# Low parts of four weight blocks made on GpSimd at their first use, and two gate products moved behind the fourth pair of heads

## The chip, the cores and the metric

The kernel runs on one core of a Trainium2 chip. The metric is the device time of one execution in microseconds (us). The core has five engines that work side by side, each through its own queue in order: TensorE (PE in the profile, PEld for its weight loads), VectorE (DVE), ScalarE (ACT), GpSimd (POOL) and SyncE (SP), which here issues nearly all DMA transfers.

## The reference

A two-layer trunk over 1024 frames of 1024 channels. Cut to what matters here:

```python
def s5_mixer(u, ..., glu_w, glu_b):
    ...
    y = jax.nn.gelu(y)
    y = y * jax.nn.sigmoid(y @ glu_w + glu_b)
    return y

def mixer_ab(h, w_in, ..., w_out):
    proj = h @ w_in
    u_s5, g_s5, q, k, v, g_ret = jnp.split(proj, cuts, axis=-1)
    y_s5 = s5_mixer(u_s5, ...) * jax.nn.silu(g_s5)
    y_ret = retention(q, k, v) * jax.nn.silu(g_ret)
    return jnp.concatenate([y_s5, y_ret], axis=-1) @ w_out

def mixer_conv(h, w_in, conv_w, conv_b, ln_g, ln_b, w_out):
    a, b, g = jnp.split(h @ w_in, 3, axis=-1)
    u = a * jax.nn.sigmoid(b)
    ...
```

Layer 0 is `x = x + mixer_ab(rmsnorm(x))`, layer 1 is `x = x + mixer_conv(rmsnorm(x))`, and a last rmsnorm follows. Retention normalises each head over its 128 channels: `(out - mu) * rsqrt(var + EPS)`. All is float32.

## The kernel before

**Products in three parts.** Every large product of float32 matrices is made as three passes over numbers split in a high and a low part: high x high, high x low, low x high (lines 277, 278 and 279, function `mm3`). A weight block of 1024 x 128 so needs two tiles, `wh` (a rounding copy, made by ScalarE) and `wl` (the rest, `wf - wh`). A pass of TensorE is one block of weights against one half `h` of the frames (512): 8 x 3 = 24 matmuls of 128 x 512 into one bank of PSUM. Three banks serve these passes in turn (`ps_mm`). A pass can begin when the bank of three passes before has been read.

**Where `wl` comes from.** The list `wseq` (function `plan`) names all weight blocks in the order of use; `wnext` hands out the next one and starts the loads of two more. `wload` then has three ways: `wload_pieces` loads `wf`, casts it on ScalarE (L268) and subtracts on GpSimd or VectorE (L269); `wload_again` loads `wf`, casts it (L146) and loads `wl` ready made from DRAM (L155); a third makes sums. Layer 1's blocks `cb0` to `cb7` and `ca0` to `ca7` (the halves b and a of `w_in`) are each used twice, once for each half of the frames. Their low parts are made beforehand and kept in DRAM (`lo_cb..`, `lo_ca..`), so both uses go by `wload_again`. `weight_low` makes half of such a block: load 256 KB (`lf`), cast on ScalarE (`lh`, L233), subtract (L234), store 256 KB (L237). There are 32 halves, numbered k = 0 to 31; k // 4 is the number of the block pair, so k = 0 to 7 are cb0, ca0, cb1 and ca1. Eighteen (`LOWS`) are made on GpSimd during the first three pairs of retention heads, and fourteen on VectorE in the gate stage behind the fourth pair: two after each pass (nb, 0) with nb of 2 to 6, one after each (nb, 1) with nb of 2 to 5. There they use two buffers in turn.

**The stage around the change.** `ret_heads` treats the retention heads in four pairs: the products of scores and values (`ro`, L1170 and L1174), statistics and roots on VectorE and ScalarE (L1183, L1184, L558, L559), normalised tiles `on` (L1194), transposes on TensorE (`rt`, L1200), and the products with the retention gate (`grl`, L1205; the last one is `last_turn`). The fourth pair lies among the first passes of the S5 gate (`mm_glu`): the order of TensorE there is written by hand. The passes run (0,0), (1,0), (0,1), (1,1), then (2,0), (2,1) to (5,1), then (6,0), (7,0), (6,1), (7,1), as (nb, h). For each, GpSimd makes `yg` = gs x yn from two loads (L1281; two buffers), ScalarE takes tanh of the bank (L1294), and VectorE makes `sg` = (sg + 1) x yg (L1298). Operands of these passes are the y tiles that `load_split` casts (L1221) and subtracts (L1223). The matrices of the output projection follow (`w_out_first`), then layer 1 with `ab(0)`: passes cb0, ca0, cb1, ca1 and so on for the first half of the frames (`mm_b`, `mm_a`), then a convolution whose taps are shared between VectorE (L1510) and GpSimd (L1490, products by ScalarE, L1489).

**What sets the order.** Instructions are traced with a priority (the program's order, or `self.at(...)`), and a planner that simulates the engines writes each engine's queue. `tc.issue_after(ins)` puts the instructions of its block behind `ins` in the queue of the engine of `ins`, without a semaphore; `chained` does the same one by one.

Of the kernel before, what the change touches and what calls it, by code (L numbers as in the profile page):

```python
# [33 lines left out]
LO_V = {f"g{i}" for i in range(1, 10)} | {"u4", "u5", "u6"}  # L34
G0 = 3
TP = 6
LOWS = 18
Y_ORDER = tuple(range(8)), (0, 2, 4, 6, 5, 7, 1, 3)
AHEAD = (0, 1, 2)
P_ORDER = ([(1, nb) for nb in range(4)] + [(2, nb) for nb in range(4)] +  # L40
# [18 lines left out]
class Trunk:  # L59
# [61 lines left out]
    def wload(self, src, name):  # L121


        if name[0] == "V":
            return self.wload_value(name)
        if src is None:
            return self.wload_sums(name)
        key, twice = name[:-2], name[:2] in TWICE and name[:-2] + "_1" in self.wnames
        if twice and key in self.lo_d:
            return self.wload_again(src, name, self.lo_d[key])  # L130
        tiles = None
        with self.at(190000) if name == "cg3_0" else nullcontext():
            for tiles in self.wload_pieces(src, name, 1, [self.nc.vector if name[:2] in LO_V or name[:3] in LO_V else self.nc.gpsimd]):
                done = tiles or done
        if twice and name.endswith("_0"):
            self.lo_d[key] = self.dram.tile([P, D], F32, name=f"lo_{key}")
            self.nc.sync.dma_start(self.lo_d[key], done[1][:].rearrange("p k n -> p (k n)").bitcast(F32))
        return done
# [803 lines left out]
    def retention(self, st):  # L942
        nc, A = self.nc, self.A
        r0 = self.r0 = self.pool("ret0", 1, stack=st)
        early = ExitStack()
        rq = self.rq = self.pool("retq", 1, stack=early, side="right")
        self.vt = [[(r0 if d else rq).tile([P, 4, HALF], F32, name=f"v{d}_{h}") for h in range(2)] for d in range(2)]
        self.rk = rq.tile([P, 2, T], F32, name="ropek")
        nc.sync.dma_start(self.rk[:], A["rope_k"])
        for i in range(2):  # L950
            for c in (slice(0, HALF), slice(HALF, T)):
                nc.gpsimd.tensor_tensor(self.rk[:, i, c], self.rk[:, i, c], self.R[:, c], op=ALU.mult)
        self.mask = r0.tile([P, 4, 64], F32, name="retmask")
        nc.sync.dma_start(self.mask[:], A["ret_mask"])
        self.g64 = r0.tile([P, 4], F32, name="g64")
        nc.sync.dma_start(self.g64[:], A["ret_g64"])
        self.kdec = r0.tile([P, NH], F32, name="kdec")
        nc.sync.dma_start(self.kdec[:], A["ret_kdec"])
        self.reps = r0.tile([P, NH], F32, name="reteps")
        nc.sync.dma_start(self.reps[:], A["ret_eps"])  # L960
        first = self.ret_proj(0)
        next(first)
        for pair in range(4):
            if pair == 0:
                with ExitStack() as vst:
                    V = self.ret_values(self.pool("vp", 1, stack=vst))
                self.rp = self.pool("ret", 1, stack=st)
                cur = list(first)[-1]
                self.crossed(0)
                ry = self.pool("retl", 1, stack=early, side="right")  # L970

            def lows(n, behind):
                with self.tc.issue_after(behind.ins):
                    for k in range(n * LOWS // 6, (n + 1) * LOWS // 6) if pair < 3 else ():
                        self.weight_low(ry, k, (("la", "lb"), ("la", "lb")), 3, nc.gpsimd)

            def turned():
                lows(2 * pair + 1, self.last_kt)
                if pair == 3:
                    early.close()  # L980
                    self.lp = self.pool("l1", side="right")
            lows(2 * pair, self.last_rs if pair else self.last_sum)
            ahead = pair in AHEAD and self.ret_proj(pair + 1)
            if ahead:
                next(ahead)
            cur = self.ret_heads(pair, *cur, V, turned, lambda: list(ahead)[-1] if ahead else None)
            if pair < 3:
                self.crossed(pair + 1)
# [229 lines left out]


    def split(self, src, hi, lo, eng, behind=None):  # L1220
        self.nc.scalar.copy(hi[:], src)  # L1221
        with self.tc.issue_after(behind.ins) if behind else nullcontext():
            eng.tensor_tensor(lo[:], src, hi[:].bitcast(F32), op=ALU.subtract)  # L1223

    def layer0_back_and_layer1(self, st):
# [37 lines left out]
        v.tensor_scalar(hgb[:], self.vecs[:, V_GLUB * KB:(V_GLUB + 1) * KB], 0.5, None, op0=ALU.mult)  # L1263
        ys_in = load_split(self.yn_d, "y", False)
        ys0, sg0, t2f, t3f, passes = {}, {}, {}, {}, {}
        left = iter(range(LOWS, 32))

        def lows(n):
            for k in islice(left, n):
                with self.tc.issue_after(self.last_turn.ins), self.tc.issue_after(self.roots[3].ins):  # L1270
                    self.weight_low(lp, k, (("cs", "pilot"), ("cq", "sq")), 1)
        ws = {}

        for nb, h in [(0, 0), (1, 0), (0, 1), (1, 1)] + [(nb, h) for nb in range(2, 6) for h in range(2)] + [(6, 0), (7, 0), (6, 1), (7, 1)]:
            if h == 0:
                ws[nb] = self.wnext(f"glu{nb}")
            yg = lp.tile([P, HALF], F32, name=f"yg{nb}_{h}", tag="ld", bufs=2)
            nc.sync.dma_start(yg[:], self.gs_d[rows(nb), hs(h)])
            yn = lp.tile([P, HALF], F32, name=f"yn{nb}_{h}", tag="ev", bufs=4)
            nc.sync.dma_start(yn[:], self.yn_d[rows(nb), hs(h)])  # L1280
            gp.tensor_tensor(yg[:], yg[:], yn[:], op=ALU.mult)  # L1281
            ps = self.bank(f"mm_glu{nb}_{h}", aux=False)
            for n, kb in enumerate(Y_ORDER[h]):
                behind = {(0, 1, 1): self.last_kv, (1, 1, 0): passes.get((0, 1, 2)), (0, 1, 3): self.last_ro,
                          (1, 1, 2): passes.get((0, 1, KB - 1))}.get((nb, h, n))
                with self.tc.issue_after(behind.ins) if behind else nullcontext():
                    self.mm3(ps[:], ws[nb], kb, (ys_in[h][kb][0][:], ys_in[h][kb][1][:]), n == 0, n == KB - 1)
                passes[nb, h, n] = self.last_mm
                self.after_pass({(0, 0, 4): self.third_turns[0], (1, 0, 2): self.third_turns[2],
                                 (1, 0, 4): self.third_turns[3], (1, 1, 1): self.second_scores, (1, 1, 6): self.turns[0], (2, 0, 5): self.turns[2],  # L1290
                                 (2, 1, 0): self.turns[3]}.get((nb, h, n)))
            sg = lp.tile([P, HALF], F32, name=f"sg{nb}_{h}", tag="u", bufs=5)
            with self.tc.issue_after(self.roots[1].ins) if (nb, h) == (0, 1) else nullcontext():
                last_sg = nc.scalar.activation(sg[:], ps[:], AF.Tanh, scale=0.5, bias=hgb[:, nb:nb + 1])  # L1294
            if nb < 2 and nb != h:
                self.chained([self.roots[2 * h]], last_sg)
            with self.tc.issue_after(self.masked[1].ins):
                v.scalar_tensor_tensor(sg[:], sg[:], 1.0, yg[:], op0=ALU.add, op1=ALU.mult)  # L1298
            if h == 0:
                a, b = (self.op_tile(opB, "B0", f"ys{q}{nb}") for q in "hl")  # L1300
                nc.scalar.mul(a[:], sg[:], 0.5)
                glu_end = v.scalar_tensor_tensor(b[:], sg[:], 0.5, a[:].bitcast(F32), op0=ALU.mult, op1=ALU.subtract)
                ys0[nb], sg0[nb] = (a, b), sg
                lows(2 if nb > 1 else 0)
                continue
            yr1 = lp.tile([P, HALF], F32, name=f"yr1_{nb}", tag="tp", bufs=TP)
            nc.sync.dma_start(yr1[:], self.yr_d[rows(nb), hs(1)])
            t3f[nb], t2f[nb] = (opB.tile([P, HALF], F32, name=f"{n}_{nb}", tag="B1") for n in ("t3f", "t2f"))
            v.scalar_tensor_tensor(t3f[nb][:], sg[:], -0.5, yr1[:], op0=ALU.mult, op1=ALU.add)
            glu_end = v.scalar_tensor_tensor(t2f[nb][:], sg0.pop(nb)[:], 0.5, t3f[nb][:], op0=ALU.mult, op1=ALU.add)  # L1310
            lows(1 if 1 < nb < 6 else 0)

        def operand(name, tag, f):
            a, b = (self.op_tile(opB if tag[0] == "B" else self.opA, tag, f"{name}{q}") for q in "hl")
# [505 lines left out]
```

## Time and profile before

| | us |
|---|---|
| median of 3 runs | 1181.55 |
| lowest, highest | 1178.34, 1181.92 |
| profiled execution | 1182.31 |
| its span, first to last instruction | 1180.4 |
| mean granted clock of TensorE | 0.995 |

The stages of that execution, as busy time of each engine in stretches of the span (the two gate stretches hold the fourth pair of heads and the gate passes):

| stretch (us) | TensorE | VectorE | ScalarE | GpSimd | clock | DMA share |
|---|---|---|---|---|---|---|
| 500 to 550 | 50.0 | 36.6 | 17.3 | 37.2 | 1.00 | 0.78 |
| 550 to 600 | 44.5 | 36.2 | 18.6 | 19.6 | 0.93 | 0.86 |
| 600 to 700 | 94.5 | 68.1 | 48.0 | 30.5 | 0.98 | 0.67 |
| 700 to 800 | 100.0 | 76.5 | 51.3 | 43.0 | 1.00 | 0.79 |
| 800 to 900 | 100.0 | 96.4 | 64.9 | 91.2 | 1.00 | 0.54 |
| 1100 to 1180 | 72.7 | 35.7 | 43.1 | 36.3 | 0.99 | 0.64 |

A row of a timeline gives start, duration, engine, line, operation, tiles and count, and in brackets the idle time of the engine before it with what ended it. DMA share is the mean busy share of the 16 DMA engines. A matmul's end in the profile is modelled: ends overlap the next start.

### The profile page before, as it was taken

What the parts mean: (1) busy time and instruction counts of PE and PEld (TensorE: products, weight loads), DVE (VectorE), ACT (ScalarE), POOL (GpSimd) and SP (SyncE); (2) the same over time, 40 slices, a digit from 0 to 9 for tenths busy, and PEclk for the clock granted to TensorE, in tenths of its full rate; (3) what the DMA queues carried; (4) which work ended last, traced back from release to release, by engine and by line L of the source; (5) the groups of instructions that cost most, each with busy time, mean ns of one, the idle gap of its engine ahead of it and who ended that gap; (6) DMA issues with size and microseconds to landing.
All of it is one profiled execution on the core that took longest, in us unless ns stands there. A gap on an engine that the chain in (4) does not pass through costs nothing.

```text
span 1180.4 us, 18518 instructions
## 1 busy us (share of the span) xinstructions
PE 1157.6 (98%) x6662; PEld 961.0 (81%) x6662; DVE 898.6 (76%) x1517; ACT 542.8 (46%) x819; POOL 714.2 (61%) x509
## 2 busy tenths in 40 slices
PE   8999999999999999998998999999999999999997
PEld 7888888888888888887776888888887888888877
DVE  7875789999615567668746787779999999999633
ACT  7212343332226643133433644467756578544662
POOL 2049999888841255476333034438894689977742
PEclk9999999999999999999899999999999999999999
DMA  9353378878888878888886666975448654457864
GB/s 342 108 175 111 134 271 314 271 270 273 268 297 299 266 224 286 213 260 275 266 292 214 205 214 218 352 255 185 161 159 295 222 180 133 133 182 239 281 229 149
DMA packets 135547, 272.17 MB, mean 231 GB/s; under 512 B 13216, under 2 KB 46368, under 8 KB 135328
## 3 DMA queue, kind: packets, MB, share of 16 engines
q1 hardware_dynamic: 134304, 266.80, 68.1%
q10 hardware_dynamic: 1152, 4.19, 0.9%
q8 instruction: 52, 0.85, 0.3%
q14 instruction: 39, 0.32, 0.1%
HBM read 192.89 MB, written 71.76 MB: 224 GB/s over the span
## 4 chain that ended last, share of the span: by engine, by line
PE 85%; DMA 5%; DVE 5%; POOL 2%; issue 2%; ACT 1%; SPq 0%; DVEq 0%; POOLq 0%; ACTq 0%
PE mm_g L278 7%; PE mm_g L279 7%; PE mm_g L277 7%; PE mm_w L277 3%; PE mm_w L278 3%; PE mm_w L279 3%; PE mm_u L279 2%; PE mm_oc L279 2%; PE mm_u L278 2%; PE mm_oc L278 2%; PE mm_oc L277 2%; PE mm_u L277 2%; PE mm_a L279 2%; PE mm_a L278 2%; PE mm_a L277 2%; PE mm_b L278 2%
## 5 line engine op out<-in xcount | busy, mean ns | idle before, releaser
L1510 DVE SCALAR_TENSOR_TENSOR cv<-u,convw,cv 128x512 f32<-128x512 f32 x358 | 244.6, 748 | 4.3 <-ACT cv L1496 2.8
L1490 POOL TENSOR_TENSOR tp<-tp,tp 128x512 f32<-128x512 f32 x104 | 138.7, 1336 | 28.9 <-ACT tp L1489 23.6
L279 PE MATMUL mm_g<-xh,wl_g 128*128 128x512 f32 x256 | 100.8, 394 | 0.0
L278 PE MATMUL mm_g<-xl,wh_g 128*128 128x512 f32 x256 | 100.6, 393 | 0.0
L277 PE MATMUL mm_g<-xh,wh_g 128*128 128x512 f32 x256 | 100.4, 392 | 0.0
L1489 ACT ACTIVATE tp<-u,convw 128x512 f32<-128x512 f32 x104 | 69.6, 714 | 9.8 <-POOL tp L1490 9.6
L277 PE MATMUL mm_glu<-yh,wh_glu 128*128 128x512 f32 x128 | 52.6, 411 | 5.5 <-ACT sg L1294 5.5
L278 PEld LDWEIGHTS mm_g<-xl,wh_g 128*128 128x128 f32 x256 | 48.1, 188 | 11.3 <-issue 1.6
L279 PEld LDWEIGHTS mm_g<-xh,wl_g 128*128 128x128 f32 x256 | 48.0, 188 | 10.5
L277 PEld LDWEIGHTS mm_g<-xh,wh_g 128*128 128x128 f32 x256 | 48.1, 188 | 9.6
L279 PE MATMUL mm_oc<-zh,wl_woc 128*128 128x512 f32 (+1 forms) x152 | 54.5, 359 | 0.9 <-DMA wl_woc<-lo_woc 0.9
L277 PE MATMUL mm_oc<-zh,wh_woc 128*128 128x512 f32 (+1 forms) x152 | 54.3, 361 | 0.0
L278 PE MATMUL mm_oc<-zl,wh_woc 128*128 128x512 f32 (+1 forms) x152 | 54.0, 356 | 0.0
L1281 POOL TENSOR_TENSOR yg<-yg,yn 128x512 f32<-128x512 f32 x16 | 21.8, 1366 | 51.0 <-DMA yg<-gs_d 33.7
L279 PE MATMUL mm_glu<-yh,wl_glu 128*128 128x512 f32 x128 | 51.7, 404 | 0.0
L278 PE MATMUL mm_glu<-yl,wh_glu 128*128 128x512 f32 x128 | 51.7, 404 | 0.0
L278 PE MATMUL mm_u<-xl,wh_u 128*128 128x512 f32 x128 | 50.0, 391 | 0.8 <-DVE xl L396 0.8
L279 PE MATMUL mm_a<-h1h,wl_ca 128*128 128x512 f32 x128 | 50.1, 391 | 0.6 <-DMA wl_ca<-lo_ca 0.6
L277 PE MATMUL mm_u<-xh,wh_u 128*128 128x512 f32 x128 | 49.2, 396 | 1.2 <-ACT xh L395 0.8
L277 PE MATMUL mm_g<-h1h,wh_cg 128*128 128x512 f32 x128 | 50.3, 393 | 0.0
L277 PE MATMUL mm_a<-h1h,wh_ca 128*128 128x512 f32 x128 | 50.2, 392 | 0.0
L279 PE MATMUL mm_b<-h1h,wl_cb 128*128 128x512 f32 x128 | 50.2, 392 | 0.0
(813 smaller groups left out, 3630.2 us busy)
## 6 DMA issues: line engine op xcount, KB each, us to landing
wf_g<-w_ab SPq DMA_DIRECT2D x16, 512.0 KB, 5.1
a<-w_out SPq DMA_DIRECT2D x32, 256.0 KB, 4.6
ws<-a SPq DMA_DIRECT2D x32, 256.0 KB, 4.7
lf<-w_c SPq DMA_DIRECT2D x32, 256.0 KB, 4.9
wf_p<-ws SPq DMA_DIRECT2D x16, 512.0 KB, 4.0
wf_cb<-w_c SPq DMA_DIRECT2D x16, 512.0 KB, 5.2
wf_ca<-w_c SPq DMA_DIRECT2D x16, 512.0 KB, 5.1
wl_cb<-lo_cb SPq DMA_DIRECT2D x16, 512.0 KB, 3.5
```

What stands on the lines that cost most here:

```text
L277: nc.tensor.matmul(ps, wh[:, kb, :], xh, start=start, stop=False)
L278: nc.tensor.matmul(ps, wh[:, kb, :], xl, start=False, stop=False)
L279: self.last_mm = nc.tensor.matmul(ps, wl[:, kb, :], xh, start=False, stop=stop)
L1281: gp.tensor_tensor(yg[:], yg[:], yn[:], op=ALU.mult)
L1489: nc.scalar.mul(sk[:], u[:, k:k + HALF], cw[:, nb, k:k + 1])
L1490: gp.tensor_tensor(s0[:], s0[:], sk[:], op=ALU.add)
L1510: v.scalar_tensor_tensor(dst[:], *tap, accs_[i][:], op0=ALU.mult, op1=ALU.add)
```

## The change

1. The halves k = 0 to 7 are no longer made beforehand (`FIRST = 8`). The eighteen made during the first three pairs of heads are now k = 8 to 25.
2. Behind the fourth pair six are left (k = 26 to 31), two each after the passes (2,0), (3,0) and (4,0), in place of fourteen.
3. Since cb0, ca0, cb1 and ca1 then have no low part in DRAM at their first use, `wload` takes the way of `wload_pieces` for them: `wf`, cast, a GpSimd subtract of the whole block (128 x 1024), and then a store of 512 KB to `lo_cb0` and so on, from which the second use loads as before.
4. The cast of `glu2` (and only it) goes behind the last cast of the y operands in ScalarE's queue (`last_cast`).
5. The two products L1298 of the passes (0,1) and (1,1) go behind `last_turn` in VectorE's queue, not behind `masked[1]` (the second product of the scores with the decay mask) as all others.

```diff
-LOWS = 18
+FIRST, LOWS = 8, 18
...
-        with self.at(190000) if name == "cg3_0" else nullcontext():
+        with (self.at(190000) if name == "cg3_0" else
+              self.tc.issue_after(self.last_cast.ins) if name == "glu2" else nullcontext()):
             for tiles in self.wload_pieces(src, name, 1, [self.nc.vector if name[:2] in LO_V or name[:3] in LO_V else self.nc.gpsimd]):
                 done = tiles or done
...
             def lows(n, behind):
                 with self.tc.issue_after(behind.ins):
-                    for k in range(n * LOWS // 6, (n + 1) * LOWS // 6) if pair < 3 else ():
+                    for k in range(FIRST + n * LOWS // 6, FIRST + (n + 1) * LOWS // 6) if pair < 3 else ():
                         self.weight_low(ry, k, (("la", "lb"), ("la", "lb")), 3, nc.gpsimd)
...
     def split(self, src, hi, lo, eng, behind=None):
-        self.nc.scalar.copy(hi[:], src)
+        self.last_cast = self.nc.scalar.copy(hi[:], src)
...
-        left = iter(range(LOWS, 32))
+        left = iter(range(FIRST + LOWS, 32))
...
-            with self.tc.issue_after(self.masked[1].ins):
+            with self.tc.issue_after((self.last_turn if h and nb < 2 else self.masked[1]).ins):
                 v.scalar_tensor_tensor(sg[:], sg[:], 1.0, yg[:], op0=ALU.add, op1=ALU.mult)
...
-                lows(2 if nb > 1 else 0)
+                lows(2 if 1 < nb < 5 else 0)
                 continue
...
-            lows(1 if 1 < nb < 6 else 0)
```

## The prediction

> **What bounds the kernel now.** I read the busy times first, then the waits of TensorE, then its timeline around each wait.
>
> ```profile
> PE 1157.6 (98%) x6662; PEld 961.0 (81%) x6662; DVE 898.6 (76%) x1517; ACT 542.8 (46%) x819; POOL 714.2 (61%) x509
> ```
> ```profile
> PE mm_glu L277 <- ACT sg L1294: 5.5, 2, 4.2
> PE ro L1174 <- issue: 3.2, 1, 3.2
> PE rt L1200 <- DVE on L1194: 2.3, 1, 2.3
> ...
> PE mm_a L279 <- DMA wl_ca<-lo_ca: 0.6, 1, 0.6
> ```
>
> TensorE is busy 98% of the span; the change takes no product away, so it can only win idle time of TensorE and time at a low clock. Columns of the waits: total us, times, longest. The three longest rows make 11.0 us, and all lie between 555 and 640 us, the stage that the change touches. The timeline of TensorE (start, duration, then the instruction) shows what each costs; the second fence is one stretch of the windows view, with the granted clock in the last column but two.
>
> ```profile
> 576.59 0.63 PE L1200 MATMUL rt<-ident,on 128*128 128x128 f32 x4 [2.34 <-DVE on L1194]
> ```
> ```profile
> 575.00:580.00 5.00, 3.41 (x13) 2.78 (x14) 5.00 (x14) 0.62 (x2) 4.46 (x3) 0.76 0.64 195
> ```
> ```profile
> 620.04 0.50 PE L277 MATMUL mm_glu<-yh,wh_glu 128*128 128x512 f32 x1 [1.30 <-ACT sg L1294]
> 620.38 0.39 PE L278 MATMUL mm_glu<-yl,wh_glu 128*128 128x512 f32 x1
> ```
> ```profile
> 635.42 0.63 PE L277 MATMUL mm_glu<-yh,wh_glu 128*128 128x512 f32 x1 [4.20 <-ACT sg L1294]
> 635.85 0.63 PE L278 MATMUL mm_glu<-yl,wh_glu 128*128 128x512 f32 x1
> ...
> 639.17 0.39 PE L277 MATMUL mm_glu<-yh,wh_glu 128*128 128x512 f32 x1
> 639.41 0.39 PE L278 MATMUL mm_glu<-yl,wh_glu 128*128 128x512 f32 x1
> 639.63 0.39 PE L279 MATMUL mm_glu<-yh,wl_glu 128*128 128x512 f32 x1
> ```
>
> A matmul of this size starts 0.23 us after the last one at full clock (639.17 to 639.63 are two such steps) and 0.43 us after it in the slow stretch behind a wait (635.42 to 635.85). Behind the 4.20 us wait that lasts from 635.42 to 639.17: 3.75 us for nine matmuls that take 9 x 0.23 = 2.05, so 1.7 us are lost on top. Behind the 2.34 us wait the clock falls too, to 0.76 in its stretch; as an estimate I take the same 1.7. Behind the 1.30 us wait the step is back at 0.23 by the second matmul: nothing. A wait is also about 0.16 longer than its row says, since a matmul's end is drawn 0.39 behind its start and the next could start after 0.23.
>
> The rule against it: the Trainium skill (TensorE: Matmul & The Clock Gate, Part 1, "What's actually happening") lets the clock fall only after an idle window of about 3.4 us. By it the 2.34 us wait would cost no slow stretch and the sum below would be 1.7 smaller; the trace shows that stretch, and I go by the trace.
>
> **Part 1: the two gate products (0,1) and (1,1), L1298, go behind the last turned head on VectorE.** Today, on VectorE and ScalarE:
>
> ```profile
> 573.20 1.76 DVE L1298 SCALAR_TENSOR_TENSOR sg<-sg,yg 128x512 f32<-128x512 f32 x1 [6.13 <-POOL yg L1281]
> 574.88 0.23 DVE L559 RECIPROCAL rs<-rs 128x4 f32<-128x4 f32 x2
> 575.08 1.36 DVE L1194 TENSOR_SCALAR on<-ro,mv,rs 128x128 f32<-128x128 f32 x4
> ```
> ```profile
> 569.37 0.48 ACT L558 ACTIVATE rs<-mv,reteps 128x4 f32<-128x4 f32 x2
> ```
>
> The roots were there at 569.85. The reciprocals and the normalisation stand behind a product that waits 6.13 us for GpSimd's yg. With the product moved, they start at 569.9: 0.23 + 1.36 for the third tile, 0.6 for a turned product, 1.36 for the fourth tile, all done by 573.6, before the transposes' place at 576.59 - 2.34 = 574.25. So the wait goes, with its slow stretch: 2.34 + 0.16 + 1.7 = **4.2 us**. What is late next: the two products wait for the last turned product, at some 578 instead of 573.2 and 578.8. Behind them queue the reuse of the two yg buffers and, through SP and GpSimd, the next yg, up to 5 us later. TensorE does not read it: a pass needs only the bank that the tanh (L1294) has read, three banks back, 2 x 5.5 us later, so I cost this at nothing; without that cover it is up to 5 us.
>
> **Part 2: eight fewer low parts behind the heads on VectorE (14 to 6).** The tanh that frees a bank stands on ScalarE behind the cast of such a low part, which waits for its load:
>
> ```profile
> 633.22 0.62 ACT L233 CAST lh<-lf 128x512 fp32r<-128x512 f32 x1 [2.66 <-DMA lf<-w_c]
> 633.74 1.04 ACT L167 CAST wh_p<-wf_p 128x1024 fp32r<-128x1024 f32 x1
> 634.69 0.68 ACT L1294 ACTIVATE sg<-mm_glu,hgb 128x512 f32<-128x512 f32 x1
> ```
> ```profile
> L233 ACT CAST lh<-lf 128x512 fp32r<-128x512 f32 x14 | 8.6, 618 | 29.0 <-DMA lf<-w_c 28.9
> ```
> ```profile
> L234 DVE TENSOR_TENSOR lh<-lf,lh x14: 675/692/1779, 582.8 to 638.1; 128x512 fp32r<-128x512 f32 x14
> ```
>
> ScalarE stood 28.9 us for these loads between 565 and 655 (the group's row), and I put the 1.30 us wait down to the same cause. The parts use two buffers in turn, so they are a chain: subtract, store, load, cast. From the first subtract (582.8) to the last (638.1) run six rounds of two, (638.1 - 582.8) / 6 = 9.2 us a round. Six parts are two rounds behind the first: begun at 579, they end near 579 + 18 = 597. The two waits are at 620 and 635, where no cast of this kind is left on ScalarE. They go with their stretch: (1.30 + 0.16) + (4.20 + 0.16) + 1.7 = **7.5 us**. The casts that stay stand behind tanhs of passes with some 10 us to spare each. Eight casts (0.62) and eight subtracts (0.69), and 4 MB of DMA, also leave; I count nothing for them. What is late next is the stage's own pass, 24 x 0.23 = 5.5 us.
>
> **Part 3: the low parts of cb0, ca0, cb1, ca1 made whole on GpSimd at first use.** Each goes wf, cast, one GpSimd subtract of 128x1024, and a store of 512 KB on SP's queue in place of a load of 512 KB. The nearest row for the subtract is the same line for other weights. Today's stage (GpSimd, TensorE, ScalarE, GpSimd):
>
> ```profile
> L269 POOL TENSOR_TENSOR wl_cg<-wf_cg,wh_cg 128x1024 fp32r<-128x1024 f32 x8 | 19.3, 2412 | 0.0
> ```
> ```profile
> L525 POOL TENSOR_TENSOR s1q<-s1q,s1q 128x512 f32<-128x512 f32 x2 | 2.8, 1398 | 2.4 <-issue 1.6 <-DMA x_d<-x 0.7
> L1449 POOL MEMSET u<- 128x30 f32 x5 | 0.6, 123 | 12.7 <-DVE xn L1423 12.2 <-DMA wl_cb<-lo_cb 0.5
> ```
> ```profile
> 771.96 0.39 PE L279 MATMUL mm_a<-h1h,wl_ca 128*128 128x512 f32 x1
> ...
> 787.82 0.39 PE L279 MATMUL mm_a<-h1h,wl_ca 128*128 128x512 f32 x1
> ```
> ```profile
> 765.27 1.04 ACT L146 CAST wh_ca<-wf_ca 128x1024 fp32r<-128x1024 f32 x1
> ...
> 781.04 1.05 ACT L146 CAST wh_ca<-wf_ca 128x1024 fp32r<-128x1024 f32 x1 [4.94 <-PE mm_b L278]
> ```
> ```profile
> 786.34 19.04 POOL L1490 TENSOR_TENSOR tp<-tp,tp 128x512 f32<-128x512 f32 x14 [11.92 <-ACT tp L1489]
> ```
>
> The second fence is all that GpSimd does from 756 to 786 us: 3.4 of 30 us. Four subtracts are 4 x 2.41 = 9.6 us, so they fit. The two ca are the tightest, since a cast waits until a pass has left its buffer. ca0: cast at 765.27, end 766.3, subtract to 768.7, first read at 771.96, 3.2 us to spare. ca1: cast at 781.04, subtract from 782.1 to 784.5, first read at 787.82, 3.3 to spare. The conv taps start at 786.34, after both. Value taken: **0**. Bounds: a gain of 0.6 at most (the last row in the list of TensorE's waits is one for such a load, somewhere in the kernel); a loss of one subtract and a slow stretch, 2.4 + 1.7 = 4.1 us, for each of the four passes, 16.4.
>
> **Part 4: glu2's cast behind the last cast of y.** It removes a block of ScalarE and VectorE, but not of TensorE:
>
> ```profile
> 555.76 1.04 ACT L268 CAST wh_glu<-wf_glu 128x1024 fp32r<-128x1024 f32 x1 [6.38 <-DMA wf_glu<-w_glu]
> 556.72 0.61 ACT L1221 CAST yh<-yf 128x512 fp32r<-128x512 f32 x1
> ```
> ```profile
> q8 instruction: 52, 0.85, 0.3%
> ```
>
> The last y cast moves ahead of a 6.38 us wait, and the head statistics come earlier with it; part 1 needs only the roots, which are chained behind the tanh of (0,1), so TensorE gains nothing: 0. The bounds are 0 and the 3.2 us stall in the heads' products with its stretch, 3.2 + 0.16 + 1.7 = 5.1, which lies at the same time. I take 0: that stall is put down to "issue", in the middle of products whose inputs had all been read, while DMA was full (next fences). It looks like TensorE waiting for its own instructions (the instruction queue moves 0.85 MB in 52 packets, the size of its program).
>
> ```profile
> 559.47 0.32 PE L1174 MATMUL ro<-vx,sc 64*64 64x128 f32 x2 [3.21 <-issue]
> ```
> ```profile
> 555.00:560.00 5.00, 1.79 (x51) 1.38 (x43) 3.52 (x5) 2.85 (x3) 2.34 (x1) 1.00 1.04 386
> ```
>
> (The last two columns are DMA share, 1.04, and GB/s.) The eighteen low parts in the heads before keep number, engine and bytes, so this window keeps its traffic.
>
> The Trainium skill (Runtime: NRT & Kernel Launch, "Instruction fetch mechanics") says that fetching is hidden by the pace of issue. By that rule the stall is a wait which the profile doesn't show, and it may go: rival A.
>
> **The sum.** 4.2 + 7.5 + 0 + 0 = 11.7 us. The profiled execution took 1182.31 us (span 1180.4; the 1.9 us around it stay): 1170.6. It lies 0.8 above the median of 1181.55, so the forecast for the median is 1169.9, rounded to **1170**. None of the three long waits lies behind 640 us, so the rest moves forward as a whole.
>
> **Rivals.**
> A. The stall before 559.47 goes too, if it hangs on the y cast (for: it lies beside that chain in time; against: the inputs were there). 11.7 + 5.1 = 16.8: 1165.
> B. One gain is given back: a low part still holds a tanh (for: the casts that stay wait for loads too), or one pass of cb or ca waits for GpSimd. 4.1 to 7.5 us: 1174 to 1177.
> C. Nothing: two or three of the four passes wait for GpSimd, 4.1 each, 8.2 to 12.3: 1178 to 1182.
> D. Slower: GpSimd works in its queue's order, and if the planner puts each of the four subtracts behind something late there (a memset that waits for xn, the sum L525, the taps), all four passes wait: 16.4 against 11.7, 1186. It decides from the fourth wait, or when each lasts over (11.7 + 3.5) / 4 = 3.8 us with its stretch. Against: 26.6 of the 30 us of GpSimd are free, and both ca have over 3 us, more than a whole subtract, to spare.
> E. The planner places the moved instructions otherwise than traced, and part 1 doesn't happen: 1174, inside B.
>
> **How the numbers follow.** Forecast 0.53 (1167.5 to 1173), A 0.12, B with E 0.20, C 0.08, D 0.07. The range 1164 to 1178 holds the forecast, A and B: about 0.83. A measurement of this kernel tells 0.3%, 3.5 us, from no change, so faster means under 1178: 0.85; same 0.08; slower 0.07.
>
> **What would show it.** Right: no TensorE wait on L1194 and none on L1294 behind 570 us, no clock under full in the gates except behind the stall at 555 to 560; casts of low parts (L233) ending before 605; four L269 rows for wl_cb and wl_ca on GpSimd before the first conv tap, and no wait of TensorE there. Wrong: a wait of mm_b or mm_a on POOL, a yg wait that reaches the tanh, or the stall growing where DMA is full.

## The result, and the profile after

| | before | changed |
|---|---|---|
| median (us) | 1180.47, 6 runs | 1166.4, 6 runs |
| lowest, highest | 1178.34, 1181.92 | 1165.22, 1168.8 |
| ratio, 95% interval | 1 | 0.9884 [0.9869, 0.99] |
| profiled execution, its span | 1182.31, 1180.4 | 1166.69, 1164.9 |

The changed kernel takes 14.1 us less; its median lies 3.6 under the forecast of 1170. Line numbers of the changed kernel are one higher from `wload` to the end of the gate passes (L1298 is L1299), and the same again in layer 1 (L1490). First the busy times of its page, then the waits of TensorE (total us, times, longest):

```profile
PE 1153.1 (99%) x6662; PEld 959.9 (82%) x6662; DVE 893.1 (77%) x1509; ACT 537.6 (46%) x811; POOL 722.0 (62%) x513
```
```profile
PE ro L1175 <- issue: 1.9, 1, 1.9
PE idle L373 <- DVE epst L318: 1.1, 1, 1.1
PE mm_oc L280 <- DMA wl_woc<-lo_woc: 1.0, 1, 1.0
PE mm_u L279 <- DVE xl L397: 0.9, 1, 0.9
```

The wait on L1194 and both waits on the tanh are gone, the stall put down to "issue" is left, and no wait on GpSimd has come in; the waits left out are of 0.6 us and less. The stretches of the changed kernel (busy time of TensorE, weight loads, VectorE, ScalarE, GpSimd, then clock, DMA share, GB/s) show a full clock everywhere in the gates but behind that stall:

```profile
555.00:560.00 5.00, 3.20 (x14) 2.48 (x14) 4.74 (x27) 2.57 (x4) 2.36 (x1) 0.84 1.03 393
560.00:565.00 5.00, 5.00 (x19) 4.04 (x19) 2.49 (x18) 2.63 (x3) 0.00 (x0) 0.82 1.05 400
...
575.00:580.00 5.00, 5.00 (x23) 4.13 (x23) 5.00 (x8) 1.41 (x3) 1.33 (x1) 1.00 0.76 214
...
620.00:640.00 20.00, 20.00 (x90) 16.57 (x89) 14.62 (x20) 9.72 (x16) 5.63 (x4) 1.00 0.61 196
```

For the time itself two marks of the timeline serve: the start of the last `ro` product, and the first product of the output projection (`mm_w`), where the gates end. Before, then changed:

```profile
559.64 0.27 PE L1174 MATMUL ro<-v,sc 64*64 64x128 f32 x1
...
648.04 0.39 PE L277 MATMUL mm_w<-ysh,wh_p 128*128 128x512 f32 x1
```
```profile
556.97 0.27 PE L1175 MATMUL ro<-v,sc 64*64 64x128 f32 x1
...
633.54 0.39 PE L278 MATMUL mm_w<-ysh,wh_p 128*128 128x512 f32 x1
```

The span fell by 15.5 us. Ahead of the first mark went 2.7, of which 1.3 is the stall (3.2 before, 1.9 now); the other 1.4 are taken up again under "What was mis-sized". Between the marks lie 88.4 us before and 76.6 now: 11.8 less, where the prediction has 11.7. The last 1.0 goes behind the second mark.

VectorE's timeline in the changed kernel, behind the roots:

```profile
567.02 0.37 DVE L560 RECIPROCAL rs<-rs 128x4 f32<-128x4 f32 x2 [4.53 <-ACT rs L559]
567.31 1.33 DVE L1195 TENSOR_SCALAR on<-ro,mv,rs 128x128 f32<-128x128 f32 x4
...
574.56 0.69 DVE L1206 TENSOR_TENSOR grl<-rt,grl 128x512 f32<-128x512 f32 x1 [1.81 <-PE rt L1201]
575.17 2.31 DVE L1299 SCALAR_TENSOR_TENSOR sg<-sg,yg 128x512 f32<-128x512 f32 x2
...
586.37 1.76 DVE L1299 SCALAR_TENSOR_TENSOR sg<-sg,yg 128x512 f32<-128x512 f32 x1 [4.68 <-POOL yg L1282]
```

The reciprocal now waits for the roots alone; the normalised tiles follow at once, and the two gate products stand behind the last turned one. The next product but one waits 4.68 us for GpSimd's yg, the lateness that the prediction named, and TensorE, busy in all of that time, doesn't see it in this profile (e9 has one where it does). The low parts that are left (tile view of `lh`: min/median/max ns, first and last start):

```profile
L234 ACT CAST lh<-lf x6: 603/610/622, 567.1 to 600.1; 128x512 fp32r<-128x512 f32 x6
L235 DVE TENSOR_TENSOR lh<-lf,lh x6: 676/680/1778, 577.4 to 604.4; 128x512 fp32r<-128x512 f32 x6
```

The last cast starts at 600.1; the chain ends at 605, where 597 was forecast: the two rounds behind the first took 27 us (577.4 to 604.4), not 18. That is still ahead of the place of the first old wait, 620. Last, GpSimd where layer 1 begins, and TensorE's first read of the second ca block's low part:

```profile
743.45 2.36 POOL L270 TENSOR_TENSOR wl_cb<-wf_cb,wh_cb 128x1024 fp32r<-128x1024 f32 x1 [0.78 <-ACT wh_cb L269]
...
751.75 2.41 POOL L270 TENSOR_TENSOR wl_ca<-wf_ca,wh_ca 128x1024 fp32r<-128x1024 f32 x1 [0.96 <-ACT wh_ca L269]
...
757.33 2.42 POOL L270 TENSOR_TENSOR wl_cb<-wf_cb,wh_cb 128x1024 fp32r<-128x1024 f32 x1 [0.48 <-ACT wh_cb L269]
...
767.53 2.40 POOL L270 TENSOR_TENSOR wl_ca<-wf_ca,wh_ca 128x1024 fp32r<-128x1024 f32 x1 [6.53 <-ACT wh_ca L269]
771.70 19.05 POOL L1490 TENSOR_TENSOR tp<-tp,tp 128x512 f32<-128x512 f32 x14 [1.77 <-ACT tp L1489]
```
```profile
773.18 0.39 PE L280 MATMUL mm_a<-h1h,wl_ca 128*128 128x512 f32 x1
```

Four subtracts of 2.4 us, all ahead of the first conv tap, each waiting for its cast and for nothing else; the last ends at 769.93, 3.2 us ahead of its read.

### The profile page after: what moved, and what is told of

It is laid out like the page before. It is cut to its first block, busy times and chain, and to the rows that moved or that the text cites. A ratio compares the mean times of both kernels' runs of the same rounds, so it can differ in the third digit from the quotient of the medians.

```text
span 1164.9 us, 18460 instructions
## 1 busy us (share of the span) xinstructions
PE 1153.1 (99%) x6662; PEld 959.9 (82%) x6662; DVE 893.1 (77%) x1509; ACT 537.6 (46%) x811; POOL 722.0 (62%) x513
## 4 chain that ended last, share of the span: by engine, by line
PE 98%; DMA 1%; DVE 0%; issue 0%; SPq 0%; POOL 0%; ACT 0%; DVEq 0%
PE mm_g L279 8%; PE mm_g L280 8%; PE mm_g L278 7%; PE mm_w L278 4%; PE mm_w L279 4%; PE mm_w L280 4%; PE mm_glu L278 3%; PE mm_glu L280 3%; PE mm_glu L279 3%; PE mm_a L280 3%; PE mm_a L278 2%; PE mm_b L278 2%; PE mm_b L280 2%; PE mm_b L279 2%; PE mm_a L279 2%; PE mm_u L280 2%
## 5 line engine op out<-in xcount | busy, mean ns | idle before, releaser
L1490 POOL TENSOR_TENSOR tp<-tp,tp 128x512 f32<-128x512 f32 x104 | 138.7, 1336 | 18.9 <-ACT tp L1489 13.6
L279 PE MATMUL mm_g<-h1l,wh_cg 128*128 128x512 f32 x128 | 49.8, 389 | 0.0
L280 PE MATMUL mm_g<-h1h,wl_cg 128*128 128x512 f32 x128 | 49.8, 389 | 0.0
```

Of the source, the lines that this page charges most:

```text
L279: nc.tensor.matmul(ps, wh[:, kb, :], xl, start=False, stop=False)
L280: self.last_mm = nc.tensor.matmul(ps, wl[:, kb, :], xh, start=False, stop=stop)
L1490: gp.tensor_tensor(s0[:], s0[:], sk[:], op=ALU.add)
```

## The experiments

Twelve kernels, in three groups (e1 to e4, e5 to e8, e9 to e12), each group timed beside the kernel before on the same chip: 1180.36 us (median of 17 runs), 1180.62 (11) and 1180.07 (7).

### e1: the two products alone

```diff
-            with self.tc.issue_after(self.masked[1].ins):
+            with self.tc.issue_after((self.last_turn if h and nb < 2 else self.masked[1]).ins):
```

> Part 1 alone: the kernel before, with only the products of (0,1) and (1,1) put behind the last turned head. Theory (separate waits): the 2.34 us wait on L1194 and its slow stretch go, 4.2 us (ratio 0.9964); the two waits on the tanh stay at about 5.5 us in all. Rival (one chain): the fourteen low parts pace the whole gate stage, so what is won at 576 us is given back at 620 and 635 us, whose waits grow to some 9 us in all: ratio 1.000.

Measured: 1174.48 us, ratio 0.9954 [0.9941, 0.9967], 1.7 us better than the 4.2 us expected; no slow stretch follows the stall in its profile, which alone is worth about that. Its waits of TensorE in the gates:

```profile
PE mm_glu L277 <- ACT sg L1294: 5.0, 2, 3.1
PE ro L1174 <- issue: 2.6, 1, 2.6
```

The wait on L1194 is gone and the tanh waits stay (5.0 us for 5.5): the gain is the products' own, and the two parts of the change are no single chain.

### e2: the low parts alone (parts 2 and 3)

```diff
-LOWS = 18
+FIRST, LOWS = 8, 18
...
-                    for k in range(n * LOWS // 6, (n + 1) * LOWS // 6) if pair < 3 else ():
+                    for k in range(FIRST + n * LOWS // 6, FIRST + (n + 1) * LOWS // 6) if pair < 3 else ():
...
-        left = iter(range(LOWS, 32))
+        left = iter(range(FIRST + LOWS, 32))
...
-                lows(2 if nb > 1 else 0)
+                lows(2 if 1 < nb < 5 else 0)
...
-            lows(1 if 1 < nb < 6 else 0)
```

> Parts 2 and 3 alone: eight low parts made at first use, six left behind the heads; products and glu2's cast as before. Theory (separate waits): the waits on the tanh and the stretch behind the second go, 7.5 us (ratio 0.9936), the wait on L1194 stays at 2.3 us, and first use costs nothing. Rival (one chain): the whole 11.7 us come from here (ratio 0.9901).

Measured: 1172.69 us, ratio 0.9944 [0.9931, 0.9956]. The waits, and the stretch behind the first of them:

```profile
PE rt L1200 <- DVE on L1194: 4.1, 1, 4.1
PE ro L1174 <- issue: 1.7, 1, 1.7
```
```profile
575.00:580.00 5.00, 5.00 (x17) 4.02 (x16) 4.28 (x8) 1.21 (x2) 4.05 (x2) 0.50 0.71 221
```

The tanh waits are gone, but the wait on L1194, which was to stay at 2.3 us, grew to 4.1, and the whole of this stretch ran at a clock of 0.50. (The 0.76 of before in the same stretch can't be set against it: there the slow steps begin only at 576.59.) Why the wait grew is under e5.

### e3: glu2's cast alone

```diff
-        with self.at(190000) if name == "cg3_0" else nullcontext():
+        with (self.at(190000) if name == "cg3_0" else
+              self.tc.issue_after(self.last_cast.ins) if name == "glu2" else nullcontext()):
...
-        self.nc.scalar.copy(hi[:], src)
+        self.last_cast = self.nc.scalar.copy(hi[:], src)
```

> Part 4 alone: glu2's cast behind the last cast of y. Theory: 0 (ratio 0.9985 to 1.0015), the stall put down to issue stays at 2 to 4 us. Rival (hidden wait on the y chain): the stall of 3.2 us and its slow stretch go, 5 us (ratio 0.9957).

Measured: 1176.75 us (11 runs), ratio 0.9977 [0.9969, 0.9986]: a small gain where none was expected. Its waits:

```profile
PE rt L1201 <- DVE on L1195: 5.2, 1, 5.2
PE mm_glu L278 <- ACT sg L1295: 2.7, 1, 2.7
PE ro L1175 <- issue: 1.1, 1, 1.1
```

One tanh wait of 2.7 us stands where before had two with 5.5, against a wait on `on` of 5.2 for 2.3. The fourteen low parts run in rounds of (633.8 - 582.1) / 6 = 8.6 us here, by the first and last subtract, and of 9.2 before. That an earlier cast makes these rounds shorter was not tested by itself.

### e4: the casts of the fourteen low parts on GpSimd

The kernel before, with all the low parts' traffic left as it was, but not on ScalarE:

```diff
-        self.nc.scalar.copy(hi[:], f[:])
+        if e:
+            self.nc.scalar.copy(hi[:], f[:])
+        else:
+            self.nc.gpsimd.tensor_copy(hi[:], f[:])
```

(`e` is given for the eighteen in the heads; their casts stay on ScalarE.)

> The kernel before, with all fourteen low parts behind the heads, but their casts (L233) on GpSimd in place of ScalarE; loads, stores and subtracts stay. Theory (the tanh stands behind a cast that waits for its load, in ScalarE's queue): the waits on the tanh fall under 1 us in all though the traffic is the same, ratio 0.993 to 0.996, less what GpSimd's own queue (yg, low parts of glu) then holds up. Rival (it is the traffic, or VectorE's subtracts, that hold the stage): the waits on the tanh stay over 4 us, ratio 0.999 or more.

Measured: 1174.05 us, ratio 0.9946 [0.993, 0.9961].

```profile
PE rt L1203 <- DVE on L1197: 3.8, 1, 3.8
PE ro L1177 <- issue: 1.9, 1, 1.9
```

All fourteen parts are still made, still loaded and still stored, and the tanh waits are gone. The casts now wait for their loads on GpSimd, and the last subtract starts later than before (641.0 against 638.1). So it was the cast in ScalarE's queue that held the tanh, not the DMA traffic of the parts.

### e5: the changed kernel without the products' move

The edit of e1, undone.

> The changed kernel without part 1 (the two products where they were). Theory: the wait on L1194 comes back and is longer than the 2.3 us of before, 4 to 6 us, because the yg load that the product waits for lands at the time DMA sets, however early TensorE is; with a slow stretch of 1.7. So it is 6 to 7 us slower than the changed kernel: ratio 0.994 against the kernel before. Rival (part 1 is worth its 4.2 everywhere): ratio 0.992.

Measured: 1172.52 us, ratio 0.9935 [0.9916, 0.9954], by the ratio what was expected; the wait is 3.85 us, a little under the 4 to 6 expected. TensorE's wait, and the work of GpSimd that ends it in this kernel, in before and in the changed one:

```profile
574.63 0.63 PE L1201 MATMUL rt<-ident,on 128*128 128x128 f32 x4 [3.85 <-DVE on L1195]
```
```profile
569.94 2.50 POOL L1282 TENSOR_TENSOR yg<-yg,yn 128x512 f32<-128x512 f32 x2 [10.81 <-DMA yg<-gs_d]
```
```profile
571.88 2.53 POOL L1281 TENSOR_TENSOR yg<-yg,yn 128x512 f32<-128x512 f32 x2 [12.65 <-DMA yg<-gs_d]
```
```profile
569.08 2.55 POOL L1282 TENSOR_TENSOR yg<-yg,yn 128x512 f32<-128x512 f32 x2 [10.84 <-DMA yg<-gs_d]
```

The wait is back, longer than before. yg is set by its load, for which GpSimd waits until 12.1 us behind the last `ro` product here (569.94 - 557.79, the start of that product), 12.2 before (571.88 - 559.64) and 12.1 in the changed kernel. That end stands still. What moved is TensorE: its first transposes came 7.2 us behind the last `ro` product here and in e2, against 8.8 before, since no slow stretch followed the stall in these two profiles. With the products ahead of the roots, TensorE can't keep what it wins in front of this load: 1.5 us more of waiting (3.85 against 2.34) for 1.6 us won.

### e6: the changed kernel without the cast's move

The edit of e3, undone.

> The changed kernel without part 4 (glu2's cast where it was). Theory as predicted (the roots that matter are chained behind the tanh of (0,1), so the y cast holds nothing of TensorE): same as the changed kernel, ratio 0.988 to 0.990. Rival (part 4 is worth what it gave alone, some 2.8 us): ratio 0.991.

Measured: 1169.61 us, ratio 0.9912 [0.9894, 0.9931]; the stall is 2.4 us, no other wait in the gates. Some 3 us slower than the changed kernel, by the rival's ratio; but between the two marks its profile takes 76.4 us, as the changed kernel's (76.6), and its excess lies ahead of the gates (the last `ro` product starts at 560.31, there at 556.97). e10 puts it to the test again.

### e7: the loads of yr held behind those of yg

```diff
-            nc.sync.dma_start(yg[:], self.gs_d[rows(nb), hs(h)])
+            yg_load = nc.sync.dma_start(yg[:], self.gs_d[rows(nb), hs(h)])
...
-            nc.sync.dma_start(yr1[:], self.yr_d[rows(nb), hs(1)])
+            with self.tc.issue_after(yg_load.ins):
+                nc.sync.dma_start(yr1[:], self.yr_d[rows(nb), hs(1)])
```

> The changed kernel with the loads of yr (L1308) behind the load of yg of the same pass in SP's queue, so that some 1 to 1.5 MB of prefetch leave the stretch from 549 to 562 us where DMA is full. Theory (the stall put down to issue is TensorE's instructions arriving late through a full DMA): the stall of 1.9 us falls under 1 us and the slow stretch behind it goes in most runs, 2 to 3.5 us faster than the changed kernel, ratio 0.986. Rival (a hidden wait that has nothing to do with DMA): stall 1 to 3 us, ratio 0.988 to 0.989.

Measured: 1165.83 us, ratio 0.9881 [0.9865, 0.9898], where 0.986 was expected; the stall is 1.4 us, where under 1 was expected.

```profile
550.00:555.00 5.00, 5.00 (x99) 4.27 (x101) 4.65 (x13) 1.71 (x3) 4.28 (x4) 1.00 1.02 376
555.00:560.00 5.00, 3.62 (x83) 3.03 (x75) 4.86 (x22) 2.90 (x4) 2.36 (x1) 1.00 1.03 389
```

The DMA share at the stall stayed at 1.02 and 1.03, so the edit didn't thin the traffic that it was meant to thin, and says nothing on the stall.

### e8: six blocks at their first use, none behind the heads

```diff
-FIRST, LOWS = 8, 18
+FIRST, LOWS = 12, 20
```

> The changed kernel with k = 0 to 11 at first use (cb2 and ca2 too), twenty in the heads before and none behind the fourth pair. Theory: nothing is left on the tanh to win, and the two further subtracts (4.8 us) meet the conv taps on GpSimd, which shows as idle time of VectorE in the convolution but not on TensorE: ratio 0.986 to 0.990. Rival (GpSimd in first use delays a pass): one or two waits of mm_b or mm_a, each 4.1 us with its slow stretch, ratio 0.991 to 0.995.

Measured: 1167.85 us, ratio 0.9901 [0.9883, 0.9919], its interval around the changed kernel's ratio. No pass of cb or ca waits for GpSimd with six blocks either, so part 3 had room left (a wait of 1.2 us on GpSimd, for the sum of the norm ahead of these passes, also stands in e4, 1.1 us, which makes no block at first use); and no more is to be won by taking the last low parts out of the gates.

### e9 and e10: the changed kernel again, and once more without the cast's move

> The changed kernel once more, as the measure for the three beside it on the same chip: ratio 0.987 to 0.990.

> The changed kernel without part 4 once more, beside the changed kernel. Theory as predicted: no difference, under 1 us. Rival (part 4 is worth about 3 us, as in the two runs that took it alone and away): 2 to 4 us over the changed kernel, ratio 0.990 to 0.992.

Measured side by side: 1167.5 us, 0.9896 [0.9881, 0.9911], with the cast's move, and 1167.25 us, 0.9895 [0.9877, 0.9912], without it. The 3 us of e6 did not come again: in the changed kernel part 4 is worth nothing that can be measured. The profile of e9 shows one wait in the gates that the first profile of the same kernel didn't have. The row of the waits, then the rows that lead to it, from VectorE, ScalarE and TensorE:

```profile
PE mm_glu L278 <- ACT sg L1295: 1.3, 1, 1.3
```
```profile
588.54 1.76 DVE L1299 SCALAR_TENSOR_TENSOR sg<-sg,yg 128x512 f32<-128x512 f32 x1 [5.70 <-POOL yg L1282]
...
599.55 0.63 ACT L1302 ACTIVATE ysh<-sg 128x512 fp32r<-128x512 f32 x1 [7.49 <-DVE sg L1299]
...
601.02 0.68 ACT L1295 ACTIVATE sg<-mm_glu,hgb 128x512 f32<-128x512 f32 x1
...
601.75 0.50 PE L278 MATMUL mm_glu<-yh,wh_glu 128*128 128x512 f32 x1 [1.31 <-ACT sg L1295]
```

VectorE waits 5.70 us for yg, 4.68 in the first profile, and then works without a gap up to the product for which ScalarE's `ysh` waits; the tanh stands behind that. So here the late yg does reach the tanh, which the prediction names among its signs of being wrong. In the first profile the same tanh ends at 599.66 and the pass begins at 600.90: 1.2 us to spare, in a profile where the slow stretch behind the stall had made TensorE 1.6 us later.

### e11 and e12: ten warm-up products fewer at the start

At its start the kernel runs fourteen warm-up products of 128 columns, whose results nothing reads (28 records, 5.5 us in the changed kernel's profile); four of 448 (8 records) take about as long, 5.1 us. Nothing else is touched (e12 has the edit of e7 besides):

```diff
-WARM = 14
+WARM = 4
...
+        wide = ev.tile([P, 448], F32, name="wide")
+        nc.vector.memset(wide[:], 1.0)
...
-            nc.tensor.matmul(idle[:, :P], self.ones[:], self.ones[:], start=True, stop=True)
+            nc.tensor.matmul(idle[:, :448], self.ones[:], wide[:], start=True, stop=True)
```

> The changed kernel with the fourteen warm-up matmuls of 128 columns (28 records) at the very start of TensorE's queue made as four of 448 columns (8 records): TensorE's program is shorter by 20 pairs of load and matmul ahead of everything else, and the start takes as long. Theory (the stall is TensorE waiting for the next block of its own program, so it belongs to a place in the instruction stream): the stall leaves the product at which it stood in every run so far, five before the end of the last heads, and moves 20 records on, some 15 large matmuls or 3.4 us further, where it is under 0.5 us or gone, with its slow stretch: 2 to 3.5 us faster than the changed kernel, ratio 0.986. Rival (a wait that belongs to these products): it stays at the same product, 1 to 3 us, same time.

> The kernel with the shorter warm-up and also the loads of yr behind those of yg. Theory: the same as with the shorter warm-up alone, within 1 us, since nothing else waits in that stage; ratio 0.985 to 0.987. Rival (holding yr back gives a gain of its own): 1 us or more faster than the shorter warm-up alone.

Measured: e11 1167.68 us, 0.99 [0.9885, 0.9914]; e12 1166.14 us, 0.9884 [0.9869, 0.9899]. (Each of these products leaves two records, so their number falls by 20, from 6662 to 6642; the counts below are of records.) e11 is no faster than the changed kernel beside it (e9), where 2 to 3.5 us were expected. In its profile the stall at the fourth pair is gone, two others stand in earlier pairs, and the tanh is waited for as in e9:

```profile
458.47 0.33 PE L1177 MATMUL ro<-v,sc 64*64 64x128 f32 x2 [0.74 <-issue]
...
530.09 0.33 PE L1177 MATMUL ro<-v,sc 64*64 64x128 f32 x2 [1.10 <-issue]
```
```profile
PE mm_glu L278 <- ACT sg L1297: 1.3, 1, 1.3
```

e12 is 1.5 us below e11, which is the rival's size, but the two intervals overlap. Its profile has no wait on the tanh (0.41 us on L1197 instead), nor has that of e7: in these two VectorE waits 2.3 and 3.5 us for yg at the place of the 5.70 above, and 4.0 to 5.7 in the six other profiles with parts 1 and 2. So the held loads of yr do let yg come earlier; that this is worth time is not shown.

A stretch from the span's start to a stall counts the products (x, first bracket) and weight loads (second bracket) ahead of it. Before and the changed kernel, up to the stall at the fourth pair; then e6, whose third pair has a stall of 0.9 us too; then e11, up to its two stalls:

```profile
0.00:559.47 559.47, 552.90 (x3906) 461.37 (x3907) 402.87 (x767) 200.46 (x303) 348.26 (x247) 1.00 0.75 245
```
```profile
0.00:556.79 556.79, 552.85 (x3906) 462.12 (x3907) 401.57 (x778) 199.99 (x303) 346.77 (x247) 1.00 0.75 245
```
```profile
0.00:527.75 527.75, 524.84 (x3526) 438.29 (x3526) 378.04 (x696) 187.88 (x282) 325.70 (x230) 1.00 0.74 244
```
```profile
0.00:458.46 458.46, 455.02 (x2765) 375.52 (x2765) 328.67 (x533) 172.75 (x255) 288.65 (x204) 1.00 0.73 246
0.00:530.09 530.09, 525.53 (x3526) 435.03 (x3526) 379.88 (x703) 189.86 (x285) 327.80 (x232) 1.00 0.74 244
```

Every stall of this kind over 0.3 us between 430 and 600 us, in all fourteen profiles, stands behind 2765, 3526 or 3906 products. In e6 the product behind the 3526th is an `ro` with `S` and `qrot`; in e11, whose program is 20 records shorter ahead of that place, it is another one. What stays the same is the count. The steps are 761 and 380: the second is half the first. So the stall belongs to a place in TensorE's instruction stream and not to a product, a buffer or a transfer that the product reads.

What is waited for there, the DMA records of the traces show. The queue q8 carries instructions; over the span it moves 52 packets of 16 KB, one for each 6662 / 52 = 128 records of products, so that the steps of 761 and 380 are, nearly, six and three packets. The view of the DMA queues of before has one of them between 557 and 558.1 us (packets, MB, share of the 16 engines):

```profile
q8 instruction: 1, 0.02, 5.5%
```

The stretches from 545 to 557 and from 558.1 to 563 us have none. By its record that packet lands at 558.04, and the product behind the stall starts at 559.47, 1.4 us later. So it is at all twenty stalls: each ends 1.25 to 1.60 us behind the landing of a packet of q8, be the stall 0.3 or 3.2 us long. In the other 22 of the 42 times that a profile passes one of the three places, the last packet had landed 1.87 to 3.82 us ahead, and TensorE doesn't stall. So the stall is TensorE waiting for its next instructions. This is read from the order of times in fourteen profiles; no run moved a packet by itself, and what makes a packet late is open. A full DMA is not needed for it: in the half microsecond before the stall's end the DMA share is 0.96 to 1.06 for eighteen of the twenty, but 0.44 and 0.32 for the second stalls of e11 and e12.

Moving the place away from the fourth pair won no time: e11 stalls 1.8 us in all, e9 beside it 2.1.

## Why the prediction was right

**The terms add up.** Between the two marks, I take e7 as the floor (74.9 us: no wait in the gates, no slow stretch). To it I add each wait of the gates with 0.16, and 1.7 for each slow stretch, as the prediction priced them:

| kernel | stretch behind the stall | wait on L1194 | waits on the tanh | sum | measured |
|---|---|---|---|---|---|
| before | 1.7 | 2.34 + 0.16 + 1.7 | 1.30 + 0.16; 4.20 + 0.16 + 1.7 | 88.3 | 88.4 |
| changed, e6, e8, e10 | 1.7 | none | none | 76.6 | 76.6, 76.4, 76.5, 76.5 |
| e1 | none | none | 1.91 + 0.16; 3.12 + 0.16 + 1.7 | 82.0 | 82.2 |
| e2 | none | 4.13 + 0.16 + 2.6 | none | 81.8 | 81.9 |
| e3 | none | 5.2 + 0.16 + 1.7 | 2.71 + 0.16 | 84.8 | 85.2 |
| e4 | 1.7 | 3.8 + 0.16 + 1.7 | none | 82.3 | 82.4 |
| e5 | none | 3.85 + 0.16 + 1.7 | none | 80.6 | 80.6 |
| e9 | none | none | 1.3 + 0.16 | 76.4 | 76.6 |
| e11 | none | none | 1.35 + 0.16 | 76.4 | 76.6 |
| e12 | none | 0.41 + 0.16 | none | 75.5 | 75.5 |

(Whether a stretch is slow is read from the steps between products; e2's lasts from 574.42 to 579.85, 0.9 longer than before's from 576.59 to 581.08.) Thirteen kernels beside the floor, each within 0.4 us: the waits and the stretches behind them are all that distinguishes them in this stage.

**Part 1, 4.2 us.** Right. e5 against the changed kernel gives 80.6 - 76.6 = 4.0 between the marks; e5's profile has no slow stretch behind the stall and the changed kernel's has, and with that made equal it is 80.6 - 74.9 = 5.7. By medians it is 5.0 to 6.1 (1172.52 against 1167.5 and 1166.4), with overlapping spreads. The lateness of yg that comes with it was priced at nothing with a bound of 5 us: it is nothing in six of the eight profiles with parts 1 and 2, and a wait of 1.3 us on the tanh in e9 and e11. So the cover that the prediction counts on (three banks) is thin; that the first profile shows no such wait was luck, with 1.2 us to spare.

**Part 2, 7.5 us.** Right in the changed kernel: e1, which lacks it, stands 82.2 - 76.6 = 5.6 higher though its profile has no stretch behind the stall, 7.3 with that made equal. Alone it gives less, 88.4 - 81.9 = 6.5 in e2, of which 1.7 is the stretch behind the stall that e2's profile lacks, since the longer wait on L1194 takes 2.7 back. The mechanism is that of the text: e4 leaves the traffic and takes only the casts from ScalarE's queue, and the waits go. The pace of the six parts that stay was mis-sized (605 for 597) without a cost.

**Part 3, 0 us.** Right. The spare time was 3.2 us for the second ca, where 3.3 was worked out, and e8 shows that two more blocks fit.

**Part 4, 0 us.** Right in the changed kernel (e9 and e10). In the kernel before it is worth about 2.7 us (1180.36 x 0.0023), e3. The table says what that is: one wait on the tanh less (4.6 with its stretch and 0.16s) and a stretch behind the stall less (1.7), against 2.9 more on L1194. Why a tanh wait goes is open; with part 2 in place none is left to go.

**What was mis-sized: the whole, by 0.9 to 2.4 us.** The gain is 12.6 us by e9's group and 14.1 by the first runs, for 11.7. The forecast moves everything ahead of the gates by nothing; in the two profiles it is 2.7 us, and their marks place it. Before the first low part (its cast starts at 443.8 in the changed kernel) 0.9 is there already: the first product of the values (`mm_v`) starts at 353.7 before, at 352.8 in the changed kernel and at 353.5 in e9, which is the same kernel again. Some 0.5 comes by 531 us, where before has a small stall at 457.16 (0.31 us by its row) that the changed kernel's profile lacks. The last 1.3 is the stall at the fourth pair, which measures 1.4 in the changed kernel's second profile, 2.6 in e1 and 1.1 in e3, with no order by what the kernels contain. That any of these 2.7 us is the change's doing isn't shown. Of the 1.0 us behind the second mark 0.6 is a wait on a load of `wl_ca` at 913.49 in before, and e10 has one like it (0.4).

**Rivals.** A, that the stall hangs on the y cast and goes, did not come: with the cast moved it is 1.9, 1.7, 1.4, 2.1, 1.4 and 1.1 us, without it 3.2, 2.6, 1.7, 1.9, 2.4 and 1.8, and in all twelve it stands behind the 3906th product and ends behind a packet of q8. The means, 1.6 and 2.3, differ by less than the values on either side do, so a part of it, some 0.7 us, is neither shown nor excluded. The rule of the Trainium skill that lent A some weight (Runtime: NRT & Kernel Launch, "Instruction fetch mechanics") has the pace of issue hide fetching; the traces disagree here, with twenty stalls of 0.3 to 3.2 us that end 1.25 to 1.60 us behind a packet of instructions. B came neither by a low part nor by a pass of layer 1 (e9's 1.3 us came by yg), C and D did not come: no row of `mm_b` or `mm_a` waits for GpSimd. E, the planner placing the products otherwise, is ruled out by VectorE's rows from 574.56 on.

## What to carry to other kernels

An operation that waits for a transfer should not stand in a queue ahead of one that another engine waits for: both gains came from that, one on ScalarE (a cast that waited for its load, ahead of the tanh that frees a bank) and one on VectorE (a product that waited for yg, ahead of the heads' normalisation). Such gains need not be independent: where the end of a wait is set by a transfer, as that on L1194, the wait grows when TensorE comes earlier (2.3 to 4.1 us in e2), so an experiment that leaves it in reads low; e1, which takes it away, doesn't. And what is moved back in a queue makes something else late: that needs a look in more than one profile, since the first showed no wait where two others have 1.3 us. A wait of the engine that bounds the kernel costs more than its row says, here 0.16 us and often 1.7 us of low clock.

## What the runs showed of the hardware

**When the clock falls.** Behind waits or stalls of 1.8 (e10), 1.9 (e4 and the changed kernel), 2.1, 2.34, 2.4 us and all of 3.1 and more the clock fell, and behind those of 1.1 to 1.7 it didn't; but neither did it behind 1.91 us (e1's first tanh wait), 2.6 (e1's stall) and 2.7 (e3's tanh wait, whose stretch follows):

```profile
630.00:635.00 5.00, 3.88 (x17) 3.23 (x18) 4.71 (x7) 2.28 (x4) 1.27 (x1) 1.00 0.58 175
```

So length alone doesn't decide, and what does is open. The Trainium skill (TensorE: Matmul & The Clock Gate, Part 1, "What's actually happening") calls the window in which activity is watched free-running, which could make the place of a wait in it count. The idle window of about 3.4 us that the Trainium skill gives in the same section is longer than the waits of 1.8 to 3.2 us that had a slow stretch here, and no run shows the window itself.

**A stall at a fixed count of instructions.** Behind 2765, 3526 and 3906 recorded products of TensorE, 0.3 to 3.2 us long, where TensorE starts a product every 0.03 us. It ends 1.25 to 1.60 us behind the landing of a 16 KB packet of the instruction queue. This was not expected, and where it falls moves with every instruction added or taken out ahead of it.
